# Moving half of a subtraction from VectorE to GpSimd for two resident operands of a transformer layer

## The chip, the cores and the metric

The kernel runs on one core of one Trainium2 chip. A core has five engines that run their own instruction queues and meet through semaphores: TensorE (PE in the profile; PEld is its weight load), VectorE (DVE), ScalarE (ACT), GpSimd (POOL) and SyncE (SP), which here issues nearly all DMAs. Working memory is SBUF (128 partitions); TensorE writes its sums to PSUM, in banks of 128x512; the inputs, the outputs and the intermediate results of the stages lie in HBM and are moved by DMA. The metric is the time of one execution on the device, in microseconds (us).

## The reference

One layer for 2048 tokens of width 1024, in float32: a token mixing step (sliding-window attention beside a gated linear recurrence), cross-attention into 256 memory tokens, and a SwiGLU feed-forward block of width 2816, each between two RMS norms with a residual.

```python
u = rms_norm(h, g_mix_pre)
z = u @ w_in                                   # 1024 x 2816
ya = swa_with_sinks(...)                       # columns of z
yh = hgrn2(...)                                # the others
y = concatenate([ya, yh]) @ w_out
h = h + rms_norm(y, g_mix_post)
u = rms_norm(h, g_x_pre)
m = rms_norm(mem, g_mem)
# cross-attention, 4 heads of 256, 256 memory tokens
q, k, v = u @ wq, m @ wk, m @ wv
y = (softmax(q k^T / 16) v) @ wo
h = h + rms_norm(y, g_x_post)
u = rms_norm(h, g_ffn_pre)
y = (silu(u @ w_gate) * (u @ w_up)) @ w_down
h = h + rms_norm(y, g_ffn_post)
```

## The kernel before

**Stages.** The first stage projects the tokens with `w_in`; the second runs the two kinds of token mixing and, beside them, folds the memory into two matrices: `qk` = wq k^T (1024x1024, heads by memory tokens) and `vo` = v wo. From there on one function, `phases` (line 1210), runs eight jobs one after the other, each a large matrix product: job 0 `w_out` (8 blocks of 256 tokens), job 1 the scores with `qk` (8 blocks), job 2 the values with `vo` (8), jobs 3 and 4 the hidden layer for the first and the second 1024 tokens (22 blocks each, 11 pairs of gate and up columns), jobs 5 to 7 the down projection in three slices of its depth. In every job one operand is *resident*: it stays in SBUF for all blocks. In job 1 that is `qk`, in job 3 the first half of the normalised tokens, transposed. The other operand is *streamed*, block by block.

**Seven products and three passes.** A block of a job is normally made as seven products in the manner of Strassen and Winograd (`seven`, line 1126): the resident operand is present as seven *parts*, sums and differences of its quarters, numbered 1 to 7, and a block uses them in the order 1, 5, 6, 3, 7, 2, 4. A last block of each job is made by quarters (`eight`) and uses an eighth part instead of some. Each part is held as two numbers, hi (the value rounded to the format of TensorE's faster float32 matmul) and lo = raw - hi, the rest; a product is then three matmuls for each of four slices of 128 rows (`products`, line 1114: hi by hi at line 1122, streamed hi by resident lo at 1123, streamed lo by resident hi at 1124). A step of a block is so twelve matmuls of 128x512.

**How a part is made.** `resident` (line 992) makes a part in two halves of two slices each. For each half a raw tile of 128x1024 is loaded to a buffer named `row`; then `split2` (line 982) lets ACT write hi (line 985) and DVE subtract (line 988) to give lo. Streamed tiles (`streamed`, line 1063) go through the same two lines, with tiles named S; some of their hi copies are made by POOL (line 987). In the profile resident parts are named T, streamed ones S.

**When a part is made.** There are seven slots for parts (four in the pool `big`, three in the pool `T`). `half` (line 1262) takes the next part of a queue as soon as a slot's last use has passed; so the parts of a job are made during the last block of the job before it and during its own first block, a stretch of some 60 us. Seven of the eight are made there, the eighth later. Rows are shared: nine `row` buffers hold raw halves, outputs of blocks and residuals, and a load to a row waits until its last reader is done.

**What else runs there.** At the same time the blocks of the job before end with their norms: DVE multiplies by the gain (lines 1520, 1595, 1608) and adds the residual (1521, 1599), ACT squares and sums (1471) and copies PSUM out (1137, 1375, 1495), POOL forms 1/sqrt (`rstds`, lines 1482 to 1486, the last one a `pow`), and TensorE transposes (1374). In the score blocks POOL also scales the row maxima (1554) for ACT's exponentials (1556).

**Order.** The instruction order on each engine isn't written by hand: a scheduler places the traced instructions by its own time model, so an instruction that changes its engine can also shift others near it. Within an engine's queue the order is then fixed; an instruction that waits holds up all behind it.

Of the kernel before, what the change touches and what calls it, by code (L numbers as in the profile page):

```python
# [15 lines left out]
ALU = mybir.AluOpType  # L16
# [20 lines left out]
def f32(ap):  # L37
    return ap.bitcast(F32)
# [10 lines left out]
class Layer:  # L49
# [929 lines left out]
    TAKES = {"s": (1,) * 7, "p": (2, 2, 0, 0), "q": (4, 0), "u": (2, 2), "v": (0, 0)}  # L979
    BLOCK = {1: (0, 0), 8: (0, 1), 2: (1, 0), 3: (1, 1)}  # L980

    def split2(self, raw, hi, lo, engine):

        if engine == "A":
            self.nc.scalar.activation(hi, raw, AF.Copy)  # L985
        else:
            self.nc.gpsimd.tensor_scalar(hi, raw, 1.0, 1.0, ALU.mult, ALU.mult)  # L987
        self.nc.vector.tensor_tensor(lo, raw, f32(hi), ALU.subtract)  # L988

    CHAIN = (5, 7, 6, 4)  # L990

    def resident(self, get, nk, key, dst, keep, sums):

        nc = self.nc
        halves = [(0, (nk + 1) // 2), ((nk + 1) // 2, nk)]

        def fetched(a, b):
            if key in self.BLOCK:  # L1000
                return get(*self.BLOCK[key], a, b - a), None
            if sums:
                return get(key, None, a, b - a), None
            if key == 5:
                return get(0, 1, a, b - a), get(0, 0, a, b - a)
            if key == 7:
                return get(1, 1, a, b - a), get(0, 1, a, b - a)
            if key == 6:
                return keep[7][len(src)], get(0, 0, a, b - a)
            return get(1, 0, a, b - a), keep[6][len(src)]  # L1010

        def split(a, b, t, o):
            if o is not None:
                nc.vector.tensor_tensor(t, t, o, ALU.add if key == 6 else ALU.subtract)
            self.split2(t, dst[:, 0, a:b], dst[:, 1, a:b], "A")

        src = []
        for a, b in halves:
            t, o = fetched(a, b)
            src.append(t)  # L1020
            if key in (6, 7):
                keep[key] = src
            yield lambda a=a, b=b, t=t, o=o: split(a, b, t, o)
# [186 lines left out]
    def phases(self, jobs, first, prologue=None):  # L1210
# [9 lines left out]
        for g, (n, i, p) in enumerate(steps):  # L1220
            key = (n, p, i > len(jobs[n][2]) // 2 if p == 8 else 0)
# [6 lines left out]
        T, keep = {}, [{} for _ in jobs]  # L1228
        current, left = [None], {}
        pending = []  # L1230
        if first:
            for i, p in enumerate(first):
                k = (0, p, False)
# [5 lines left out]
        def fetch(n, tile):  # L1239
            def get(i, j, a, c):  # L1240
                t = tile().rearrange("p (k d) -> p k d", d=512)[:, :c]
                if j is None:
                    self.load(t.rearrange("p k d -> p (k d)"), jobs[n][3][self.CHAIN.index(i), :, a * 512:(a + c) * 512])
                else:
                    jobs[n][0](t, i, j, a, c)
                return t

            return jobs[n][0] if first else get

        def lag(k):  # L1250
            return 2 if k[1] in self.BLOCK or jobs[k[0]][3] is not None else 0
# [10 lines left out]
        def half(g, tile):  # L1262

            if current[0] is None:
                if not queue:
                    return False
                free = min(slots, key=lambda s: s[1])
                if free[1] > g:
                    return False
                n, p, _ = k = queue.pop(0)  # L1270
                slots.remove(free)
                slots.append((free[0], uses[k][-1], free[2]))
                self._n += 1
                dst = (self.big if free[0] == "A" else self.tb).tile(
                    [P, 2, 4, 512], F32R, tag="big" if free[0] == "A" else "T", name=f"T_{self._n}",
                    bufs=4 if free[0] == "A" else 3)[:, :, :jobs[n][1]]
                T[k] = dst
                left[k] = 2
                current[:] = [(k, self.resident(fetch(n, tile), jobs[n][1], p, dst, keep[n], jobs[n][3] is not None)), 0]
            k, f = current[0]  # L1280
            pending.append((g + lag(k), k, next(f)))
            current[1] += 1
            if current[1] == 2:
                next(f, None)
                current[0] = None
            return True

        class Ready(dict):


            def __getitem__(_, p):
                q = next(q for q in range(g, len(steps)) if steps[q][2] == p)
                n, i, _ = steps[q]
                key = (n, p, i > len(jobs[n][2]) // 2 if p == 8 else 0)
                while left.get(key, 1):
                    if not split(len(steps)):
                        assert half(g - 1, self.row_tile), (g, key, queue[:3], slots)
                return T[key]
# [18 lines left out]
        if not first:  # L1317
            for i in range(8):
                half(-1, prologue)
                split(len(steps))  # L1320
                yield
# [9 lines left out]
        for _, nk, bl, _, beside in jobs:  # L1331
            for i, (kind, _, out, follow, addend) in enumerate(bl):
                stream(at + 1)
                after += [f() for f in beside.get(i, ())]
                run = (self.seven(ready, Ready(), nk, out, addend) if kind == "s" else
                       self.eight(ready, Ready(), nk, out) if kind == "p" else
                       self.plain(ready, Ready(), nk, out, addend, kind))
                for q in range(len(self.STEPS[kind])):
                    for _ in range(1 if g or not first else 3):
                        next(run)  # L1340
                        if first and g < 3:
                            yield
                    self.mark()
                    upto(need[g + 2])
                    if first and g == 1:
                        yield
                    for _ in range(1 if kind == "s" else 2):
                        for f in list(after):
                            if next(f, after) is after:
                                after.remove(f)  # L1350
                        if pending and lag(pending[0][1]):
                            with self.behind():
                                split(g)
                        else:
                            split(g)
                        if not first or g > 1:
                            half(g, self.row_tile)
                    g += 1
                after.append(follow())
                at += 1  # L1360
# [394 lines left out]
```

## Time and profile before

| | |
|---|---|
| median of three runs | 2598.62 us (2594.67 to 2599.31) |
| profiled execution | 2587.36 us, span of instructions 2585.7 us |
| TensorE busy, granted clock | 2548.3 us (99% of the span), 0.998 |
| DVE busy | 1747.9 us (68%) |
| ACT busy | 1261.0 us (49%) |
| POOL busy | 428.4 us (17%) |
| line 988 on DVE, resident parts made from rows | 120 instructions, 141.3 us |

The span is the time from the first to the last instruction. Busy times of different engines overlap. The rows of a timeline give start, duration, engine, line, operation, the tiles (written, then read), the shapes, and in brackets how long the engine was idle before and what released it. "x2" is two instructions merged to one row. Names of tiles are without their numbers, so a T in a row can be any part; which one it is follows from the order of instructions in the queue.

### The profile page before, as it was taken

The numbers are of one execution on the slowest core, as the hardware profiler recorded it, in microseconds if no ns is written. First come the engines' busy times: TensorE is split into PE (matmuls) and PEld (weight loads), VectorE is DVE, ScalarE is ACT, GpSimd is POOL, SyncE is SP. The second block draws the span as 40 slices with busy tenths as digits, with TensorE's granted clock in tenths as the row PEclk, the third lists the DMA queues.
The fourth block names the chain that finished last, engine by engine and source line by source line (L and its number), as shares of the span: only waits on it lengthen the run. The fifth ranks groups of instructions, "written<-read, shape, count | busy, mean of one in ns | idle before, by whom it ended". The sixth has DMA issues, their size and how long they took to land.

```text
span 2585.7 us, 34998 instructions
## 1 busy us (share of the span) xinstructions
PE 2548.3 (99%) x12371; PEld 2135.9 (83%) x12371; DVE 1747.9 (68%) x2759; ACT 1261.0 (49%) x2633; POOL 428.4 (17%) x612
## 2 busy tenths in 40 slices
PE   9999999999999999999999999999999999999998
PEld 8888888888988778888878888888888888888886
DVE  7785588986557778788876655576566556564656
ACT  5563466665555566465563333353333334443543
POOL 5231334321302232222300000000000000000022
PEclk9999999999999999999999999999999999999999
DMA  6445655855888886666963622253565444566888
GB/s 188 147 163 179 198 168 152 253 185 167 258 290 281 296 287 210 205 222 210 327 233 115 203 97 75 98 203 124 177 205 194 146 146 139 208 201 186 262 213 218
DMA packets 363663, 506.03 MB, mean 196 GB/s; under 512 B 20960, under 2 KB 249312, under 8 KB 363488
## 3 DMA queue, kind: packets, MB, share of 16 engines
q1 hardware_dynamic: 357440, 481.77, 56.5%
q0 software_dynamic: 6048, 22.02, 4.7%
q8 instruction: 97, 1.59, 0.2%
q14 instruction: 78, 0.64, 0.1%
HBM read 337.00 MB, written 166.72 MB: 195 GB/s over the span
## 4 chain that ended last, share of the span: by engine, by line
PE 83%; DMA 7%; DVE 4%; ACT 3%; issue 2%; POOL 1%; SPq 0%; DVEq 0%; POOLq 0%; ACTq 0%
PE psm L1122 23%; PE psm L1124 23%; PE psm L1123 22%; PE psg L156 2%; PE psg L157 2%; PE psg L158 2%; PE pss L1374 1%; DMA row<-y_d 1%; DMA raw<-in_wo_x_dram 1%; DMA u_d<-row 1%; DMA h1t_d<-row 1%; DMA row<-h_d 1%; ACT junk L1471 1%; ACT T L985 0%; PE pss L837 0%
## 5 line engine op out<-in xcount | busy, mean ns | idle before, releaser
L1122 PE MATMUL psm<-T,S 128*128 128x512 f32 x2695 | 1043.8, 391 | 11.0 <-ACT part L1137 6.5
L1123 PE MATMUL psm<-T,S 128*128 128x512 f32 x2695 | 1049.1, 390 | 2.1 <-DVE T L988 1.9
L1124 PE MATMUL psm<-T,S 128*128 128x512 f32 x2695 | 1038.9, 390 | 3.6 <-DVE S L988 3.6
L1122 PEld LDWEIGHTS psm<-T,S 128*128 128x128 f32 x2695 | 506.2, 188 | 120.3 <-ACT part L1137 7.0
L1124 PEld LDWEIGHTS psm<-T,S 128*128 128x128 f32 x2695 | 506.2, 188 | 110.4 <-DVE S L988 5.3
L1123 PEld LDWEIGHTS psm<-T,S 128*128 128x128 f32 x2695 | 506.5, 188 | 107.5 <-DVE T L988 4.1
L985 ACT ACTIVATE S<-sum 128x512 fp32r<-128x512 f32 (+1 forms) x314 | 188.7, 619 | 359.6 <-PE psm L1124 267.8
L988 DVE TENSOR_TENSOR S<-sraw,S 128x512 fp32r<-128x512 f32 (+1 forms) x319 | 217.0, 687 | 215.9 <-ACT S L985 201.8
L988 DVE TENSOR_TENSOR S<-sum,S 128x512 fp32r<-128x512 f32 (+1 forms) x372 | 249.7, 681 | 47.0 <-ACT S L985 31.8
L1137 ACT ACTIVATE part<-psm 128x512 f32<-128x512 f32 x273 | 161.7, 597 | 242.8 <-PE psm L1124 221.5
L985 ACT ACTIVATE S<-sraw 128x512 fp32r<-128x512 f32 (+1 forms) x272 | 167.4, 617 | 111.2 <-PE psm L1124 99.3
L1500 POOL DMA_DIRECT2D row<-y_d x28 | 25.7, 919 | 1111.4 <-DVE row L1686 1036.5
L988 DVE TENSOR_TENSOR T<-row,T 128x1024 fp32r<-128x1024 f32 (+1 forms) x120 | 141.3, 1192 | 60.9 <-ACT T L985 60.4
L1471 ACT ACTIVATE junk<-row 128x512 f32<-128x512 f32 x160 | 99.7, 625 | 60.5 <-DVE row L1493 30.0
L157 PE MATMUL psg<-u,whi 128*128 128x512 f32 x320 | 127.8, 399 | 0.0
L158 PE MATMUL psg<-u,wlo 128*128 128x512 f32 x320 | 127.1, 397 | 0.0
L156 PE MATMUL psg<-u,whi 128*128 128x512 f32 x320 | 127.1, 397 | 0.0
L985 ACT ACTIVATE T<-row 128x1024 fp32r<-128x1024 f32 x120 | 119.9, 1028 | 10.5 <-DMA row<-qk_s 3.5
L987 POOL TENSOR_SCALAR S<-sum 128x512 fp32r<-128x512 f32 x58 | 53.4, 921 | 294.6 <-PE psm L1124 237.2
L1637 DVE TENSOR_TENSOR row<-psm,part 128x512 f32<-128x512 f32 x66 | 43.7, 687 | 61.4 <-PE psm L1124 61.3
L1646 DVE TENSOR_TENSOR part<-psm,part 128x512 f32<-128x512 f32 x60 | 39.7, 687 | 62.4 <-PE psm L1124 62.2
L812 ACT ACTIVATE S<-S,w_mn 128x256 f32<-128x256 f32 (+1 forms) x128 | 63.1, 495 | 28.6 <-DVE w_mn L808 28.3
(363 smaller groups left out, 3679.1 us busy)
## 6 DMA issues: line engine op xcount, KB each, us to landing
sraw<-in_w_gate_dram SPq DMA_DIRECT2D x44, 512.0 KB, 3.7
sraw<-in_w_up_dram SPq DMA_DIRECT2D x44, 512.0 KB, 3.7
hid_d<-row SPq DMA_DIRECT2D x44, 512.0 KB, 2.7
h_d<-row SPq DMA_DIRECT2D x32, 512.0 KB, 4.8
y_d<-row SPq DMA_DIRECT2D x32, 512.0 KB, 3.3
sraw<-hid_d SPq DMA_DIRECT2D x32, 512.0 KB, 5.1
row<-y_d POOLq DMA_DIRECT2D x28, 512.0 KB, 7.1
sraw<-in_w_in_dram SPq DMA_DIRECT2D x44, 256.0 KB, 3.5
```

Of the source, the lines that this page charges most:

```text
L156: nc.tensor.matmul(ps, ah, bh, start=(i == 0), stop=False)
L157: nc.tensor.matmul(ps, ah, bl, start=False, stop=False)
L158: nc.tensor.matmul(ps, al, bh, start=False, stop=(i == n - 1))
L812: nc.scalar.activation(s[:, r, o:], s[:, r, o:], AF.Exp, bias=mn[:, i:i + 1], scale=-1.0, accum_out=den[:, i:i + 1])
L985: self.nc.scalar.activation(hi, raw, AF.Copy)
L987: self.nc.gpsimd.tensor_scalar(hi, raw, 1.0, 1.0, ALU.mult, ALU.mult)
L988: self.nc.vector.tensor_tensor(lo, raw, f32(hi), ALU.subtract)
L1122: nc.tensor.matmul(ps, s[:, 0, k, :], t[:, 0, k, :], start=st, stop=False, **kw)
L1123: nc.tensor.matmul(ps, s[:, 0, k, :], t[:, 1, k, :], start=False, stop=False, **kw)
L1124: nc.tensor.matmul(ps, s[:, 1, k, :], t[:, 0, k, :], start=False, stop=sp, **kw)
L1137: nc.scalar.activation(t, ps, AF.Copy)
L1471: self.nc.scalar.activation(junk, a, AF.Square, scale=float(D) ** -0.5, accum_out=to)
```

## The change

For job 1 and job 3, and only for the second half of each part, line 988's subtraction is issued to POOL (`nc.gpsimd`) instead of DVE. The hi copy stays on ACT. Eight parts in each of two jobs make sixteen instructions.

```diff
-    def split2(self, raw, hi, lo, engine):
+    def split2(self, raw, hi, lo, engine, rest=None):
         if engine == "A":
             self.nc.scalar.activation(hi, raw, AF.Copy)
         else:
             self.nc.gpsimd.tensor_scalar(hi, raw, 1.0, 1.0, ALU.mult, ALU.mult)
-        self.nc.vector.tensor_tensor(lo, raw, f32(hi), ALU.subtract)
+        (rest or self.nc.vector).tensor_tensor(lo, raw, f32(hi), ALU.subtract)
...
-    def resident(self, get, nk, key, dst, keep, sums):
+    def resident(self, get, nk, key, dst, keep, sums, shared):
...
-            self.split2(t, dst[:, 0, a:b], dst[:, 1, a:b], "A")
+            self.split2(t, dst[:, 0, a:b], dst[:, 1, a:b], "A", nc.gpsimd if shared and a else None)
...
-                current[:] = [(k, self.resident(fetch(n, tile), jobs[n][1], p, dst, keep[n], jobs[n][3] is not None)), 0]
+                current[:] = [(k, self.resident(fetch(n, tile), jobs[n][1], p, dst, keep[n], jobs[n][3] is not None,
+                                               n in (1, 3))), 0]
```

In the queues of the changed kernel as it is built, the moved subtractions stand on POOL behind the norms' `pow` of the same moment; around them some instructions of DVE, ACT, TensorE and SP have changed places with their neighbours, in the stretches where these two operands are made and nowhere else.

## The prediction

> **What bounds the kernel now.** I read the page's head first, then busy time by stretch for the two places where the touched parts are made, then TensorE's waits there, then the rows of the engines in those stretches.
>
> ```profile
> span 2585.7 us, 34998 instructions
> PE 2548.3 (99%) x12371; PEld 2135.9 (83%) x12371; DVE 1747.9 (68%) x2759; ACT 1261.0 (49%) x2633; POOL 428.4 (17%) x612
> ...
> 920.00:990.00 70.00, 64.66 (x304) 52.41 (x303) 54.00 (x68) 48.40 (x100) 23.00 (x29) 1.00 0.74 256
> 1270.00:1335.00 65.00, 61.84 (x282) 50.01 (x281) 54.55 (x61) 48.89 (x96) 10.17 (x16) 0.97 0.81 276
> ```
>
> TensorE is the bound. What an edit on DVE or POOL can win or lose is TensorE's idle time, and where these parts are made that is small: 70.00 - 64.66 = 5.3 us in the first stretch (columns: length, PE, PEld, DVE, ACT, POOL busy, PE clock) and 65.00 - 61.84 = 3.2 us in the second. The first holds the making of seven parts of the scores' operand, the second of seven parts of the first feed-forward operand; the eighth of each is made later. DVE is busy 77% and 84% of them.
>
> ```profile
> 959.93 0.50 PE L1123 MATMUL psm<-T,S 128*128 128x512 f32 x1 [0.92 <-DVE T L988]
> 962.76 0.47 PE L1122 MATMUL psm<-T,S 128*128 128x512 f32 x1 [1.41 <-ACT part L1137]
> 967.04 0.73 PE L1122 MATMUL psm<-T,S 128*128 128x512 f32 x2 [2.45 <-ACT T L985]
> ...
> 1305.44 0.50 PE L1122 MATMUL psm<-T,S 128*128 128x512 f32 x1 [2.04 <-ACT part L1137]
> 1306.24 0.40 PE L1122 MATMUL psm<-T,S 128*128 128x512 f32 x1
> 1306.47 0.48 PE L1123 MATMUL psm<-T,S 128*128 128x512 f32 x1
> 1306.75 0.63 PE L1124 MATMUL psm<-T,S 128*128 128x512 f32 x1
> 1309.74 0.54 PE L1122 MATMUL psm<-T,S 128*128 128x512 f32 x1
> ...
> 1323.71 0.50 PE L1123 MATMUL psm<-T,S 128*128 128x512 f32 x1 [0.24 <-DVE T L988]
> 1326.41 0.50 PE L1123 MATMUL psm<-T,S 128*128 128x512 f32 x1 [0.76 <-DVE T L988]
> ```
>
> These are the waits that an edit here can touch. Only three (0.92, 0.24, 0.76 us) end with the subtraction that moves; the large ones end with a copy or an eviction on ACT. After the 2.04 us gap matmuls start 0.23 us apart (1306.24 to 1306.47), and then 0.43: the seven from 1306.75 to 1309.74 take 2.99 us in place of 7 x 0.23, 1.4 us more. The 2.45 us gap had no such tail. The Trainium skill ("TensorE: Matmul & The Clock Gate", "What's actually happening") has the clock halve after an idle window of about 3.4 us; by that rule the 2.04 us gap alone would have had no tail, and here the row decides.
>
> **The change, part by part.** Sixteen subtractions lo = raw - hi of 128x1024 (two operands, eight parts, second halves) leave DVE and join POOL. Nothing is added or dropped; DMAs are the same in number.
>
> *Price of one.* DVE's is in the trace; POOL's of this shape isn't.
>
> ```profile
> L988 DVE TENSOR_TENSOR T<-row,T x120: 677/1218/1646, 788.6 to 2440.1; 128x1024 fp32r<-128x1024 f32 x112, 128x512 fp32r<-128x512 f32 x8
> L889 POOL TENSOR_TENSOR q<-qq,G x16: 1042/1046/2199, 268.9 to 704.8; 128x512 f32<-128x512 f32 x16
> L892 POOL TENSOR_TENSOR kk<-kk,G x16: 614/615/1164, 272.5 to 699.8; 128x256 f32<-128x256 f32 x16
> ```
>
> Two-input POOL medians are 0.615 us at 256 elements and 1.046 at 512, 0.431 us more per 256, so 1.046 + 2 x 0.431 = 1.91 us at 1024 (estimate). Ends: 1.05 us, the 512 row itself, and 2.09, its double. I take 1.91, which follows both rows. Against DVE's 1.22 each lo is 0.7 us longer once it starts. (The "GPSIMD Engine Reference" of the Trainium skill, "Elementwise — side-by-side cycle accounting", measures 4497 against 2293 ns at 2048; its ratio 1.96 would make this 2.4 us, an estimate, and add 0.5 us to each.)
>
> *Do the two engines hinder each other?*
>
> ```profile
> 1271.03 0.77 POOL L987 TENSOR_SCALAR S<-sraw 128x512 fp32r<-128x512 f32 x1 [3.38 <-PE psm L1124]
> 1271.24 1.63 DVE L988 TENSOR_TENSOR T<-row,T 128x1024 fp32r<-128x1024 f32 x1
> ...
> 961.44 4.05 POOL L987 TENSOR_SCALAR S<-sum 128x512 fp32r<-128x512 f32 x1 [5.22 <-PE psm L1124]
> ...
> 956.26 2.48 DVE L1520 SCALAR_TENSOR_TENSOR row<-row,q_r,g 128x1024 f32<-128x1024 f32 x2 [0.61 <-POOL q_r L1486]
> 958.66 2.35 DVE L988 TENSOR_TENSOR T<-row,T 128x1024 fp32r<-128x1024 f32 x2
> 960.93 2.35 DVE L1521 TENSOR_TENSOR row<-row,row 128x1024 f32<-128x1024 f32 x2
> 963.20 1.22 DVE L988 TENSOR_TENSOR T<-row,T 128x1024 fp32r<-128x1024 f32 x1
> 964.33 0.68 DVE L988 TENSOR_TENSOR S<-sraw,S 128x512 fp32r<-128x512 f32 x1
> ```
>
> They do. In the first pair DVE takes 1.63 us instead of 1.22 while a POOL copy runs; there the POOL copy took 0.77; the one at 961.44 lasts 4.05 and ends only after DVE's unbroken run of two-input work (to 965.01). So a moved subtraction first waits for DVE's current instruction (0 to 1.3 us, once 4.05 - 0.77 = 3.3), then holds DVE off for up to its 1.91 us. The Trainium skill ("SBUF — State Buffer", "Who interferes with whom") states why: a DVE instruction with two SBUF inputs and a GpSimd one that reads SBUF share one read interface, and the second to issue fully blocks. Both rows agree with it, and what it would do here is the second rival below. DVE gives up 1.13 us for each (its spacing: 960.93 to 963.20 holds two) and can be shut out for 1.91, a loss of 0.8 where it never rests. But it rests 16.0 and 10.5 us in the two stretches (70.00 - 54.00, 65.00 - 54.55), and what it loses there costs nothing.
>
> *First stretch.* The parts are used in the order 1, 5, 6, 3, 7, 2, 4.
>
> ```profile
> 949.95 0.33 SPq L75 DMA_DIRECT2D row<-qk_s  x1
> ...
> 954.23 1.06 ACT L985 ACTIVATE T<-row 128x1024 fp32r<-128x1024 f32 x1
> ...
> 957.65 8.26 DMA row<-qk_d
> ```
>
> Part 3's second lo is the first half of the pair at 958.66; its hi was ready at 955.29 (954.23 + 1.06), but two gain multiplies stood ahead, and TensorE waited 0.92 us. On POOL it follows a norm's pow and a copy of the streamed operand; with one DVE instruction to wait for it ends about 958.5 to 960.5, against 959.9. Either way the gain or loss is covered: TensorE next waits 1.41 and then until 967.04 for part 2's hi, whose raw half lands at 965.9 (957.65 + 8.26). So part 3: 0, as long as it loses under 1.41 + 2.45 us. In the changed kernel's order that load is issued ahead of a streamed tile's instead of behind it: I take 1.0 us off the 2.45 (bounds 0 and 2.45, the whole gap). Given back next: in ACT's new order the eviction that part 6 of the next block waits for stands behind part 2's second hi copy (1.06 us) and two exponentials; it was just in time before, so +1.0 (bounds 0 and 2.2). Part 2's second lo had no reserve, so it pays its 0.7, less what that eviction hides: +0.3 (bounds -0.4, its hi earlier, and 1.91). SP's raw loads wait for the moved subtractions to free their rows; the one at 949.95 followed part 6's, which is about as early on POOL: 0. Sum +0.3.
>
> *Second stretch.*
>
> ```profile
> 1283.74 1.01 POOL L1486 TENSOR_TENSOR q_r<-q_w,mhalf 128x2 f32<-128x2 f32 x1
> 1285.24 2.47 DVE L1595 SCALAR_TENSOR_TENSOR row<-row,q_r,g 128x1024 f32<-128x1024 f32 x2
> 1287.63 1.21 DVE L988 TENSOR_TENSOR T<-row,T 128x1024 fp32r<-128x1024 f32 x1
> 1288.77 2.35 DVE L1599 TENSOR_TENSOR row<-row,row 128x1024 f32<-128x1024 f32 x2
> ...
> 1290.02 0.60 ACT L1495 ACTIVATE row<-psm 128x512 f32<-128x512 f32 x1 [1.57 <-DVE row L1599]
> ...
> 1302.89 2.02 ACT L985 ACTIVATE T<-row 128x1024 fp32r<-128x1024 f32 x2
> 1304.79 1.08 ACT L1137 ACTIVATE part<-psm 128x512 f32<-128x512 f32 x2
> ...
> 1290.02:1304.79 14.77, 13.27 (x66) 10.69 (x64) 11.82 (x14) 14.74 (x31) 2.66 (x6) 1.00 0.93 322
> ```
>
> Part 1's second lo now stands on POOL right behind this pow (end 1284.75), when DVE starts the two multiplies. If it slips in between them, the first addition of L1599 ends at 1284.8 + 2 x 1.2 + 1.9 + 1.2 + 1.2 = 1291.5 instead of 1290.0; ACT waits for it and then works without rest (14.74 of 14.77 us) until the eviction at 1304.79, so the gap before 1305.44 grows by about 1.4. If DVE holds on, it shrinks by 0.4. I take +1.2. On the other side, part 3's second lo waited 4.3 us in DVE's queue (hi 1302.89 + 2.02, lo 1309.23), and its row frees this load:
>
> ```profile
> 1309.23 2.35 DVE L988 TENSOR_TENSOR T<-row,T 128x1024 fp32r<-128x1024 f32 x2
> ...
> 1310.48 6.45 DMA row<-h_d
> 1317.03 0.10 DVE row L1599
> ```
>
> On POOL it ends near 1308.5; the load, the addition, the silu and part 2's hi behind it come up to 2 us earlier, which takes the 0.24 and most of the 0.76: -0.8 (bounds -1.0, both, and 0). Part 2's extra 0.7 goes into that lead: 0. Sum +0.4.
>
> The eighth parts are made from about 1100 and 1700 on. From 1095 to 1160 TensorE's whole list of waits is one line, and from 1640 to 1760 it is empty:
>
> ```profile
> PE psm L1122 <- ACT part L1137: 0.6, 1, 0.6
> ```
>
> So they are hidden by the work of running blocks: 0. If that cover were gone each would cost its extra 0.7. POOL's norm steps and copies of the streamed operand now queue behind the moved work; they feed products or row scalings that come later than the part itself, so I give them 0 beyond the pow and multiplies counted above.
>
> Sum: 0.3 + 0.4 = +0.7 us on the profiled execution's 2587.36 (span 2585.70). The three runs' median, 2598.62, lies 11.3 above it; on that scale 2599.3. Adding all upper bounds (2.2 + 1.91 + 1.4) gives +5.5, all lower ones (-2.45 - 0.4 - 0.4 - 1.0) -4.3: the forecast's own range is 2594 to 2604. A measurement of this kernel can tell about 0.2%, 5.2 us, from no change.
>
> **Rivals.** *Slower: POOL is shut out at part 3.* DVE's run from 956.26 to 965.0 has no pause, and the row at 961.44 shows POOL kept out to the end of such a run. In the new order it loses two moved subtractions (2.3) and gains two streamed ones (1.2): to 963.9. Part 3's second lo would end at 963.9 + 1.9 = 965.8, 5.9 late; less the later waits of 1.41 and 2.45, +2.0; part 7's second lo follows on POOL, +1.9; a gap of that length brings a half-rate tail, +1.4; with the sum's 0.7 some 6 us, 2604.6. It begins to count once part 3 ends later than 959.9 + 3.9 = 963.8. For it: that row. Against: the one at 1271, where POOL came in between two DVE instructions.
>
> *Slower: DVE is shut out each time.* If DVE paces both stretches, 14 x 0.8 = 11 us: 2610. For it: loads of 54.00 + 7 x 0.8 = 59.6 us of 70 and 60.1 of 65 leave little rest. Against: the rest that is left, and that TensorE's large waits end with ACT. This is what the Trainium skill's full block (the page named above) comes to at its worst.
>
> *Faster: the gaps close.* If DVE, rid of 14 x 1.2 us, feeds ACT earlier, the 2.45 us gap goes with the earlier load and the 2.04 goes with its 1.4 tail: -5.9, 2593. For it: DVE at 84%. Against: the 2.04 gap ends with ACT, which is busy without a rest for 14 us before it.
>
> *It doesn't do what it says:* POOL merely replaces DVE as the last arriver, and nothing else moves. Same time, held in the forecast.
>
> **How the numbers follow.** Forecast (within 0.2%) 0.43; POOL shut out 0.20; DVE shut out 0.13; gaps closed 0.24. The time is the forecast's, 2599.3. The range reaches over the slow rivals' times and, by the bounds of the first stretch, some 4 us past the fast one's: 2589 to 2611 leaves about 0.2 out.
>
> **What would show it.** Right: sixteen POOL rows of L988 near 1.9 us or longer; DVE's T group down by 16; a wait of TensorE for POOL at part 2 under 1 us; the gap before the first feed-forward block's part 6 near 3 us. Wrong: POOL rows of 4 us or more at part 3 with a TensorE wait of 4 us behind them; or the two large gaps gone.

## The result, and the profile after

The changed kernel is slower: 2603.95 us median against 2596.29 for the kernel before on the same chip, ratio 1.0029 with a 95% interval of 1.0022 to 1.0037, that is 7.5 us. The profiled execution took 2597.38 us (span 2595.6), where the one before took 2587.36. Line numbers of the changed kernel are one or two higher: its matmuls are L1123 to L1125 (L1122 to L1124 before), transposes L1376 (L1374), the norms' pow L1488 (L1486), the gain multiplies L1522, L1597 and L1610 (L1520, L1595, L1608).

The head of the page, then busy time by stretch (length, PE, PEld, DVE, ACT, POOL, PE clock), both of the changed kernel:

```profile
span 2595.6 us, 35006 instructions
PE 2549.0 (98%) x12371; PEld 2135.9 (82%) x12371; DVE 1756.1 (68%) x2743; ACT 1259.5 (49%) x2633; POOL 462.5 (18%) x628
```

```profile
920.00:990.00 70.00, 63.11 (x291) 51.27 (x290) 54.66 (x53) 45.77 (x95) 31.89 (x34) 0.98 0.74 252
1270.00:1335.00 65.00, 57.93 (x272) 47.25 (x272) 53.01 (x51) 44.75 (x87) 25.91 (x20) 1.00 0.87 291
```

TensorE's busy time hardly moved (2548.3 to 2549.0); its idle time did, and in the two stretches named: 6.9 us idle instead of 5.3, and 7.1 instead of 3.2. These are 5.5 of the 9.2 us by which it grew between the two profiled executions; of the rest 1.8 us lie ahead of 900 us, where the change touches nothing, and 1.4 between 1100 and 1270, and they are not followed here. DVE was to get lighter by sixteen subtractions of 1.22 us, 19.5 us; its busy time went up by 8.2 us (1747.9 to 1756.1), and in the first stretch it issues fewer instructions (53 records for 68) in more time. The two groups of L988 that changed, by instruction group (count, shortest/median/longest in ns):

```profile
L988 DVE TENSOR_TENSOR T<-row,T x104: 678/1218/3414, 790.2 to 2449.0; 128x1024 fp32r<-128x1024 f32 x96, 128x512 fp32r<-128x512 f32 x8
...
L988 POOL TENSOR_TENSOR T<-row,T x16: 2352/2406/3381, 935.6 to 1715.7; 128x1024 fp32r<-128x1024 f32 x16
```

All sixteen moved, at a median of 2.41 us, and DVE's longest row of this kind grew from 1.65 to 3.41 us. What that does in the second stretch, rows of four engines of the changed kernel in order of time (start, duration, engine, line; in brackets the idle time before and what ended it):

```profile
1290.38 2.40 POOL L988 TENSOR_TENSOR T<-row,T 128x1024 fp32r<-128x1024 f32 x1
...
1290.45 4.61 DVE L1597 SCALAR_TENSOR_TENSOR row<-row,q_r,g 128x1024 f32<-128x1024 f32 x2 [0.91 <-POOL q_r L1488]
...
1297.36 0.60 ACT L1497 ACTIVATE row<-psm 128x512 f32<-128x512 f32 x1 [1.93 <-DVE row L1601]
...
1306.21 2.49 POOL L988 TENSOR_TENSOR T<-row,T 128x1024 fp32r<-128x1024 f32 x1 [2.82 <-ACT T L985]
...
1306.55 0.19 ACT L1473 ACTIVATION_READ_ACCUMULATOR junk<-row 128x1 f32 x1
...
1308.67 0.64 POOL L1484 TENSOR_TENSOR q_v<-q_s 128x2 f32<-128x2 f32 x1
...
1311.19 2.48 DVE L1610 SCALAR_TENSOR_TENSOR row<-row,q_r,extra 128x1024 f32<-128x1024 f32 x2 [0.60 <-POOL q_r L1488]
...
1312.62 1.06 PE L1376 MATMUL pss<-ident,row 128*128 128x128 f32 x8 [3.42 <-DVE row L1610]
...
1313.98 0.39 PE L1125 MATMUL psm<-T,S 128*128 128x512 f32 x1
1314.21 0.40 PE L1123 MATMUL psm<-T,S 128*128 128x512 f32 x1
1314.22 6.25 POOL L988 TENSOR_TENSOR T<-row,T 128x1024 fp32r<-128x1024 f32 x2
...
1314.80 3.41 DVE L988 TENSOR_TENSOR T<-row,T 128x1024 fp32r<-128x1024 f32 x1
...
1318.26 0.50 PE L1124 MATMUL psm<-T,S 128*128 128x512 f32 x1 [1.60 <-DVE T L988]
```

The same sum of squares, first small step and transposes in the kernel before:

```profile
1299.06 0.20 ACT L1471 ACTIVATION_READ_ACCUMULATOR junk<-row 128x1 f32 x1
...
1299.34 0.20 POOL L1482 TENSOR_TENSOR q_v<-q_s 128x2 f32<-128x2 f32 x1 [14.58 <-ACT junk L1471]
...
1302.33 1.06 PE L1374 MATMUL pss<-ident,row 128*128 128x128 f32 x8
```

Two things stand here. At 1290.38 part 1's subtraction starts on POOL, right behind the pow, and the two gain multiplies that the same pow releases take 4.61 us; before, the same pair took 2.47 (its row at 1285.24 in the prediction). At 1306.74 the sum of squares of the next norm is ready (1306.55 + 0.19), but POOL is in part 6's subtraction until 1308.70, so the norm's first small step starts at 1308.67, 1.9 us late; before, it followed the sum by 0.08 us. The row that both feed comes late, and TensorE, which works in its own order, waits 3.42 us ahead of its transposes; no such wait was there before. The 2.04 us gap is gone, and this one stands in its place. From 1314.22 parts 3 and 7 read on POOL, a subtraction that DVE kept takes 3.41 us for 1.22, and TensorE waits 1.60 us for it. Behind the gap of 3.42 us matmuls start 0.23 us apart (1313.98 to 1314.21): it has no half-rate tail.

The first stretch, in the same form (the pair that part 1 meets in the kernel before, then the changed kernel):

```profile
934.99 2.48 DVE L1520 SCALAR_TENSOR_TENSOR row<-row,q_r,g 128x1024 f32<-128x1024 f32 x2
```

```profile
935.58 2.40 POOL L988 TENSOR_TENSOR T<-row,T 128x1024 fp32r<-128x1024 f32 x1
...
935.64 4.62 DVE L1522 SCALAR_TENSOR_TENSOR row<-row,q_r,g 128x1024 f32<-128x1024 f32 x2 [1.78 <-POOL q_r L1488]
...
958.91 4.94 DVE L1522 SCALAR_TENSOR_TENSOR row<-row,q_r,g 128x1024 f32<-128x1024 f32 x2 [1.19 <-POOL q_r L1488]
...
959.45 3.32 POOL L988 TENSOR_TENSOR T<-row,T 128x1024 fp32r<-128x1024 f32 x1
...
962.83 0.50 PE L1124 MATMUL psm<-T,S 128*128 128x512 f32 x1 [1.37 <-POOL T L988]
...
968.92 1.29 PE L1376 MATMUL pss<-ident,row 128*128 128x128 f32 x8 [3.65 <-DVE row L1523]
...
970.56 0.63 PE L1125 MATMUL psm<-T,S 128*128 128x512 f32 x1
...
970.98 0.63 PE L1123 MATMUL psm<-T,S 128*128 128x512 f32 x1
```

Here too a pair of gain multiplies is held by part 1, at 935.6, and the next norm's by part 3, at 958.9 (2.48 us each before, the second at 956.26 in the prediction). TensorE waits 1.37 us for part 3's lo, and 3.65 us for a normed row ahead of transposes; behind that gap matmuls start 0.42 us apart (970.56 to 970.98), the half-rate tail that the prediction saw behind the 2.04 us gap.

### The profile page after: what moved, and what is told of

Its sections match the earlier page's. It is cut to its first block, busy times and chain, and to the rows that moved or that the text cites. A ratio compares the mean times of both kernels' runs of the same rounds, so it can differ in the third digit from the quotient of the medians.

```text
span 2595.6 us, 35006 instructions
## 1 busy us (share of the span) xinstructions
PE 2549.0 (98%) x12371; PEld 2135.9 (82%) x12371; DVE 1756.1 (68%) x2743; ACT 1259.5 (49%) x2633; POOL 462.5 (18%) x628
## 4 chain that ended last, share of the span: by engine, by line
PE 81%; DMA 7%; DVE 4%; issue 3%; ACT 2%; POOL 2%; SPq 1%; DVEq 0%; POOLq 0%; ACTq 0%
PE psm L1123 23%; PE psm L1125 22%; PE psm L1124 22%; PE psg L158 2%; PE psg L157 2%; PE psg L156 2%; PE pss L1376 1%; DMA row<-y_d 1%; DMA kk<-z_d 1%; DMA z<-in_w_out_dram 1%; DMA raw<-in_wo_x_dram 0%; DMA u_d<-row 0%; POOL T L988 0%; DMA x<-in_w_out_dram 0%; DMA y_d<-sg 0%
## 5 line engine op out<-in xcount | busy, mean ns | idle before, releaser
L1124 PE MATMUL psm<-T,S 128*128 128x512 f32 x2695 | 1049.6, 390 | 5.1 <-DVE T L988 3.4
L1123 PE MATMUL psm<-T,S 128*128 128x512 f32 x2695 | 1043.3, 392 | 7.8 <-ACT part L1138 5.0
L1125 PE MATMUL psm<-T,S 128*128 128x512 f32 x2695 | 1039.9, 390 | 4.3 <-DVE S L988 4.3
L1123 PEld LDWEIGHTS psm<-T,S 128*128 128x128 f32 x2695 | 506.9, 188 | 116.6 <-ACT part L1138 7.4
L1124 PEld LDWEIGHTS psm<-T,S 128*128 128x128 f32 x2695 | 506.6, 188 | 111.1 <-DVE T L988 5.0
L1125 PEld LDWEIGHTS psm<-T,S 128*128 128x128 f32 x2695 | 506.5, 188 | 111.1 <-DVE S L988 6.0
L988 DVE TENSOR_TENSOR S<-sraw,S 128x512 fp32r<-128x512 f32 (+1 forms) x319 | 221.4, 702 | 212.6 <-ACT S L985 199.9
L988 DVE TENSOR_TENSOR S<-sum,S 128x512 fp32r<-128x512 f32 (+1 forms) x372 | 255.1, 695 | 52.2 <-ACT S L985 36.2
L988 DVE TENSOR_TENSOR T<-row,T 128x1024 fp32r<-128x1024 f32 (+1 forms) x104 | 125.5, 1221 | 56.0 <-ACT T L985 55.7
L988 POOL TENSOR_TENSOR T<-row,T 128x1024 fp32r<-128x1024 f32 x16 | 41.1, 2571 | 411.6 <-ACT T L985 411.6
```

The source lines that it names most:

```text
L988: (rest or self.nc.vector).tensor_tensor(lo, raw, f32(hi), ALU.subtract)
L1123: nc.tensor.matmul(ps, s[:, 0, k, :], t[:, 0, k, :], start=st, stop=False, **kw)
L1124: nc.tensor.matmul(ps, s[:, 0, k, :], t[:, 1, k, :], start=False, stop=False, **kw)
L1125: nc.tensor.matmul(ps, s[:, 1, k, :], t[:, 0, k, :], start=False, stop=sp, **kw)
```

## The experiments

Theory A: while POOL reads for a moved subtraction, DVE's two-input work stands still; norms come late, and TensorE waits where its order puts a late row. Rival B: the planner's new order of TensorE's instructions (the transposes stand earlier) costs it. Rival C: the moved lo itself arrives late at its matmul. Rival D: POOL's queue, in which small steps now stand behind 2.4 us of other work. Every ratio is to the kernel before, run beside it.

**One operand at a time.** The edit of the first; the second has `n == 3`:

```diff
-                                               n in (1, 3))), 0]
+                                               n == 1)), 0]
```

> Only the scores' operand has its second halves subtracted by POOL; the first feed-forward operand is made as before. The trace of the changed kernel put about 2.7 us of its loss into the first stretch, 2.8 us between the stretches and 3.1 us into the second. Theory A (each POOL subtraction keeps DVE off while it reads, the norms that DVE makes come late, and TensorE waits at their transposes): a loss of its own in each stretch, so 2.7 to 5.5 us over the kernel before here, a ratio of 1.001 to 1.002, with the wait of some 3.6 us for L1523 still there. Theory B (the changed order of TensorE's instructions costs it, not DVE): the same place and the same 2.7 us, since the order around part 7 changes here as well. Theory C (the moved subtraction itself arrives late): waits for POOL's L988 add up to the loss; they were 1.4 us in the first stretch. If the loss sits in the second stretch alone: ratio 1.000.

> Only the first feed-forward operand has its second halves subtracted by POOL. Theories A and B: 3.1 us over the kernel before (ratio 1.0012), with the wait of some 3.4 us for L1610 at the transposes and the first stretch as before. By A the two parts' losses add up to that of the changed kernel, 7.5 us. By C: the waits for POOL's L988, 0.3 us in this stretch, are all of it: ratio 1.0001.

Scores' operand alone: 1.0017 (1.0006 to 1.0028). Feed-forward operand alone: 1.0012 (1.0001 to 1.0023). Together they make 1.0029, so the losses add, as far as intervals of 0.0011 to either side tell, and each stretch has its own. TensorE's waits in the first stretch of the one and the second stretch of the other:

```profile
PE pss L1376 <- DVE row L1523: 3.0, 1, 3.0
```

```profile
PE pss L1376 <- DVE row L1610: 4.6, 1, 4.6
```

Waits for POOL's own result were 1.3 and 0.3 us, less than the loss in both: C does not carry it. A and B are not told apart.

**The order of TensorE.** The changed kernel with one row tile's transposes held behind part 7's seventh matmul (`pin` is that matmul):

```diff
-                self.transposed(y[i], y[i])
+                self.transposed(y[i], y[i], pin if n == 14 and not i else ())
...
-                nc.tensor.transpose(...)
+                with self.queued(*pin): nc.tensor.transpose(...)
```

> The changed kernel, but the eight transposes of one normed row tile (the last mixed block's first) may stand on TensorE only behind the seventh of part 7's twelve matmuls, close to where they stood before the change; it moved them ahead of eleven of the twelve. Theory B: the wait of 3.6 us ahead of them and the half-rate matmuls behind it go, so 2.7 us of the 7.5 come back, ratio to the kernel before 1.0018. Theory A: the row is as late as it was; only the work that now stands ahead, six matmuls of 0.23 us, 1.4 us, comes off the wait: 2.2 us of it stay, ratio 1.0023 to 1.0029.

1.0040 (1.0025 to 1.0056): nothing came back. The transposes went back six of the eleven places that the change had moved them (5202 of TensorE's instructions stand ahead of them before, 5191 in the changed kernel, 5197 here), so this run alone does not clear the order. The traces do the rest: in both runs of the next experiment the same transposes stand at 5191, without a wait and without a loss, and in the second stretch the ones that wait stand at 6774 before as after the change. B falls. In this run the wait for the row is gone, and another took its place, larger than either theory had. POOL, DVE and TensorE, in that order:

```profile
971.54 3.15 POOL L988 TENSOR_TENSOR T<-row,T 128x1024 fp32r<-128x1024 f32 x1 [2.47 <-ACT T L985]
...
972.42 3.36 DVE L988 TENSOR_TENSOR T<-row,T 128x1024 fp32r<-128x1024 f32 x1
...
975.84 0.79 PE L1124 MATMUL psm<-T,S 128*128 128x512 f32 x1 [3.33 <-DVE T L988]
```

A subtraction that stayed on DVE is held behind one that moved, and now that is what TensorE lacks.

**POOL without the reading.** First POOL only writes (zeros in place of these lo halves; the matmuls on them start 0.23 us apart as before); then it writes two and a half times, so that it is busy as long as with the subtraction:

```diff
-        (rest or self.nc.vector).tensor_tensor(lo, raw, f32(hi), ALU.subtract)
+        if rest:   # the second run has three memsets, the last of half the tile
+            rest.tensor_tensor(lo[:, :, 0:1], raw[:, :, 0:1], f32(hi)[:, :, 0:1], ALU.subtract)
+            rest.memset(f32(lo), 0.0)
+        else: self.nc.vector.tensor_tensor(lo, raw, f32(hi), ALU.subtract)
```

> POOL in place of the moved subtractions subtracts one column of 4 or 2 elements per row and then fills lo with zeros: the writes and the wait for hi are left, nearly all of the reading and the arithmetic are left out (so lo is zero in these halves). Theory A: without the reading DVE is not held off, its pairs of gain multiplies take 2.5 us again and not 4.6, the waits of 3.6 and 3.4 us at the transposes go: no slower than the kernel before, ratio 0.998 to 1.000. Theory B: the order of the instructions is changed here as well; if it is the cause, waits of 2 us or more at the transposes stay and the ratio stays above 1.001.

> In place of each moved subtraction POOL subtracts one column (0.20 us in the run that only wrote) and then fills lo with zeros two and a half times (0.95 us each there), so about 2.5 us of POOL's time, as long as the subtraction's 2.4, with hardly any reading; lo is zero in these halves. Theory A (the reading keeps DVE off): no loss, ratio 0.998 to 1.000, DVE's pairs of gain multiplies near 2.5 us. Rival D (POOL's queue: the norms' small steps and the streamed copies stand behind 2.4 us of other work, and the reading is beside the point): the loss stays, ratio 1.002 to 1.003, with waits of 3 us at the transposes.

Written once: 0.9986 (0.9973 to 0.9999). Busy as long, without the reading: 0.9989 (0.9977 to 1.0001). The second is the test. DVE's pair and POOL's work beside it, in the second stretch:

```profile
1291.25 2.48 DVE L1597 SCALAR_TENSOR_TENSOR row<-row,q_r,g 128x1024 f32<-128x1024 f32 x2
...
1291.44 2.56 POOL L988 MEMSET T<- 128x1024 f32 x3
```

POOL is busy for 2.56 us right beside the pair, as the subtraction was for 2.40, and the pair takes 2.48 us and not 4.61. The loss is gone. POOL's queue is as full as in the changed kernel, and TensorE still waits 2.3 us for L1610 there, so D is real as a wait; without the reading it makes no net loss (the 2.04 us wait for ACT is not in that trace). The reading is the cause, together with the arithmetic on what is read, which both runs leave out with it.

**Smaller and more.** Each moved subtraction in four pieces, or done twice:

```diff
+        if rest:                          # four_pieces
+            for d in range(0, 512, 128):
+                rest.tensor_tensor(lo[:, :, d:d + 128], raw[:, :, d:d + 128], f32(hi)[:, :, d:d + 128], ALU.subtract)
+        else: self.nc.vector.tensor_tensor(lo, raw, f32(hi), ALU.subtract)
...
+        for _ in range(2 if rest else 1): # subtracted_twice
+            (rest or self.nc.vector).tensor_tensor(lo, raw, f32(hi), ALU.subtract)
```

> POOL makes each moved subtraction as four of 128x256, about 0.6 us each by the row of that width, 2.4 us in all. If a DVE instruction is held only until POOL's current instruction ends and gets in between two pieces, a pair of gain multiplies takes at most 2.5 + 2 x 0.6 = 3.7 us and the loss shrinks to about a half, ratio 1.0015. If POOL's next piece gets in first, the pair takes 4.6 us or more and the ratio stays at 1.003.

> POOL does each moved subtraction twice over (same result, 16 more reads of 2.4 us). Theory A and rival D: the loss about doubles, 15 us, ratio 1.006 (more if TensorE's gaps become long enough for a lower clock). If the loss came from the changed order alone (theory B), it stays near 7.5 us, 1.003.

Four pieces: 1.0026 (1.0015 to 1.0038). The pair shrank as the first case said, to 3.44 us, and the loss did not, as the second said. Part 1 and the pair in the second stretch, POOL and then DVE:

```profile
1297.27 5.77 POOL L988 TENSOR_TENSOR T<-row,T 128x256 fp32r<-128x256 f32 x4
...
1297.32 3.44 DVE L1597 SCALAR_TENSOR_TENSOR row<-row,q_r,g 128x1024 f32<-128x1024 f32 x2 [0.60 <-POOL q_r L1488]
```

The rows fit two engines that take turns piece by piece, so that the cost is shared out: DVE is held 1.0 us instead of 2.1, and POOL's four pieces, 4 x 0.72 us at the shortest, take 5.77. TensorE then waits 4.0 us for POOL's lo in the first stretch, in three waits (1.4 in the changed kernel), and 5.4 for L1610.

Twice: 1.0130 (1.0111 to 1.0149), some 34 us, more than four times the change's loss where twice was expected. A and D had only the sign of that. Part of the excess is TensorE's clock, which is lower in both stretches (the column before the last two; 0.98 and 1.00 in the changed kernel above):

```profile
920.00:990.00 70.00, 59.63 (x264) 47.85 (x262) 57.53 (x42) 38.34 (x76) 45.66 (x35) 0.95 0.75 253
1270.00:1345.00 75.00, 65.53 (x299) 53.18 (x298) 65.49 (x60) 47.07 (x97) 40.96 (x31) 0.95 0.84 279
```

The mean granted clock of these runs is 0.991, against 0.996 of the kernel before beside them; over 2593 us that is some 13 of the 34 us (an estimate). That the slack which takes the first reads no longer takes the second is likely for the others, and was not tried.

**The reading by itself.** DVE makes every lo as before, and POOL subtracts besides, into the dead raw half:

```diff
-        (rest or self.nc.vector).tensor_tensor(lo, raw, f32(hi), ALU.subtract)
+        self.nc.vector.tensor_tensor(lo, raw, f32(hi), ALU.subtract)
+        rest and rest.tensor_tensor(raw, raw, f32(hi), ALU.subtract)
```

> The move is undone: DVE makes every lo as before the change, and nothing that TensorE uses comes from POOL; but POOL subtracts too, behind DVE, into the raw half, which nobody reads again (the half comes free for the next load up to some 2.4 us later). Theory A: the reads keep DVE off as in the changed kernel and DVE has its old work besides: at least its 7.5 us, and about 11 with the 3.6 that the run that only wrote had gained, ratio 1.003 to 1.0045. Theories B and C (order, late lo): the consumer is as before, ratio 1.000 to 1.001.

1.0090 (1.0075 to 1.0104), some 23 us: nothing that TensorE uses was moved, and the loss is three times the change's. B and C are out as causes of the whole. It is twice what A expected. The mean granted clock is 0.9925 against 0.9969 beside it, over 2594 us some 11 us (an estimate), about what is above the expectation; that rows come free later may be part of it as well, and was not separated.

**Which parts.** By the condition on `key`: parts 1, 5 and 6; parts 3, 7, 2 and 4; the eighth alone; part 1 alone.

```diff
-            self.split2(t, dst[:, 0, a:b], dst[:, 1, a:b], "A", nc.gpsimd if shared and a else None)
+            self.split2(t, dst[:, 0, a:b], dst[:, 1, a:b], "A", nc.gpsimd if shared and a and key in (1, 5, 6) else None)
```

> POOL makes only the second half of the eighth part of either operand; the other fourteen stay with DVE, and the instructions on every engine stand nearly as before the change. By the prediction's zero for the eighth parts, and by theory A, since DVE and TensorE have other work there that covers it: ratio 1.000, 0.999 to 1.001, and TensorE's waits in the two stretches as before the change (2.5 and 2.0 us for ACT).

> POOL makes the second halves of parts 1, 5 and 6 of both operands; parts 3, 7, 2, 4 and the eighth stay with DVE. In the changed kernel's trace POOL's reads of these three lengthen DVE's work by about 2.1 + 2.0 us in the first stretch (pair of gain multiplies 4.6 for 2.5, a streamed subtraction 2.7 for 0.7) and 2.1 + 0.8 in the second, 7.0 of some 21.7 us. Theory A, if the loss goes by the time that DVE is kept off: 7.5 x 7.0 / 21.7 = 2.4 us, ratio 1.001. If these three are used early enough to have slack: 1.000 or under.

> POOL makes the second halves of parts 3, 7, 2 and 4 of both operands; the others stay with DVE. Their reads lengthen DVE's work by about 6.5 us in the first stretch and 8.2 in the second, 14.7 of some 21.7 us. Theory A: 7.5 x 14.7 / 21.7 = 5.1 us, ratio 1.002. If the early parts carry the loss: 1.000.

> POOL makes only the second half of part 1 of either operand. The run with the first three parts lost all that the changed kernel loses, and its trace offers two mechanisms: part 1's read starts right behind a norm's pow and holds the second of that norm's two gain multiplies (the pair takes 4.6 for 2.5 us, in both stretches), and part 6's stands in front of the next norm's small steps on POOL (their sums were ready at 1310.4, q_v started at 1312.28, 1.9 us later). If the held pair carries it: 2.1 us in either stretch or somewhat more, ratio 1.0015 to 1.002, with the pairs at 4.6 us and a wait at the transposes of the second stretch near 2.5 us. If part 6's place on POOL or its hold carries it: ratio 1.000 to 1.0005 and no wait for L1610 of more than 1 us.

| POOL makes | moved | ratio | interval |
|---|---|---|---|
| the eighth parts | 2 | 0.9995 | 0.9982 to 1.0007 |
| 1, 5, 6 | 6 | 1.0036 | 1.0023 to 1.0049 |
| 3, 7, 2, 4 | 8 | 1.0006 | 0.9994 to 1.0018 |
| 1 | 2 | 1.0018 | 1.0007 to 1.0028 |

The share by DVE's held time was wrong, and clearly: the four parts with two thirds of it cost nothing that can be told, the three with one third cost as much as the whole change. Two subtractions of sixteen, part 1's, make some 60% of it by the middle value; the interval reaches from a quarter to nearly all. The second stretch with part 1 alone, POOL, DVE and TensorE:

```profile
1288.06 2.39 POOL L988 TENSOR_TENSOR T<-row,T 128x1024 fp32r<-128x1024 f32 x1
...
1288.12 4.61 DVE L1597 SCALAR_TENSOR_TENSOR row<-row,q_r,g 128x1024 f32<-128x1024 f32 x2
...
1308.19 1.06 PE L1376 MATMUL pss<-ident,row 128*128 128x128 f32 x8 [2.59 <-ACT junk L1473]
```

So the held pair is enough here: 2.1 us on DVE at 1288 are a wait of 2.59 us 20 us later, at the transposes of the next norm (the profile names ACT's sum of squares in its chain as the last to come). The wait for ACT right behind them is 1.35 us, where it was 2.04, so some 1.9 us are new. With parts 5 and 6 moved as well (ACT, POOL and TensorE in the run of the first three):

```profile
1310.17 0.20 ACT L1473 ACTIVATION_READ_ACCUMULATOR junk<-row 128x1 f32 x1
...
1312.28 0.64 POOL L1484 TENSOR_TENSOR q_v<-q_s 128x2 f32<-128x2 f32 x1
...
1316.23 1.94 PE L1376 MATMUL pss<-ident,row 128*128 128x128 f32 x8 [4.73 <-DVE row L1610]
```

The sum is ready at 1310.37 and POOL takes it up at 1312.28, behind part 6's subtraction; TensorE's wait goes from 2.59 to 4.73 us. That these 1.9 us are part 6's is read from the trace; part 6 was not moved alone. In the first stretch no single part explains the loss: TensorE's listed waits from 920 to 1000 us sum to 5.2 us before, 6.9 in the changed kernel, 4.6 with part 1 alone, 6.3 with parts 1, 5 and 6 (the largest, 4.3 us, for a copy by ACT and not for L1523) and 3.5 with 3, 7, 2 and 4. Its pair is held in the run of part 1 too (4.61 us), so which holds make its 4.4 us stays open. No version that was run beats the kernel before while it computes every lo.

## Why the prediction was right or wrong

The predicted 2599.3 us is 4.7 under the measured median, and 2589 to 2611 holds it; the likeliest case, within 0.2%, did not come true. The number flatters the sum. It said +0.7 us and 7.5 were measured, outside of its own bounds of -4.3 to +5.5; the time came nearer because the three runs that it started from had a median of 2598.62, 2.3 us above that of the kernel before beside the changed one, and the range holds it because it was stretched over the slow rivals.

- **Price of one.** 1.91 us was wrong, and so was its upper end, 2.09: 2.41 measured. From 512 elements (1.046 us) to 1024 it grows by 1.36 us, where the two smaller rows gave 2 x 0.431. The ratio cited from the "GPSIMD Engine Reference" of the Trainium skill, "Elementwise — side-by-side cycle accounting", 1.96, gave 2.4 as an estimate; the trace's 2.41 / 1.22 = 1.98 agrees.
- **Do the engines hinder each other.** Right, and more than priced: a hold is POOL's whole read, 2.1 us of 2.4 on the pair, and not 0.8 net. "SBUF — State Buffer", "Who interferes with whom", in the Trainium skill says full block between two-input DVE work and a GpSimd read; the pairs of 4.61 with the reading and 2.48 with as long a write agree.
- **DVE's rest of 16.0 and 10.5 us, in which a loss costs nothing.** This is the step that failed. The rest is a sum over a stretch; what counts is which instruction is held. Parts 3, 7, 2 and 4 held DVE longest at 1.0006; part 1 held it 2.1 us, on the chain of a norm, at 1.0018.
- **First stretch, +0.3.** Measured alone: 1.0017, 4.4 us. Part 3 was followed with care and came out as said (late by little, TensorE waits 1.37 us, inside the bound); part 1, whose subtraction meets the pair at 935.6, has no term in the sum, nor has the hold of the next pair by part 3's own read. How much of the loss is each one's is not shown.
- **Second stretch, +0.4.** Measured alone: 1.0012, 3.1 us. Part 1's term had the right mechanism, POOL slipping in at the gain multiplies, and half its size: 1.2 for 2.1 on the pair and some 1.9 at TensorE. Its path was another too: the sum put it on the gap ahead of part 6, which ends with an eviction by ACT; it came at the transposes of the next norm. It starts 0.07 us ahead of the first multiply (1290.38, 1290.45), not between the two. Of the gain of 0.8 from part 3's earlier row a part can be seen: at the same two matmuls the wait of 0.24 is 0.30 (now for POOL) and that of 0.76 is no longer listed, with TensorE itself later. But two new waits for subtractions that DVE kept, 1.60 and 1.75 us, stand ahead of them, where there was none.
- **POOL's norm steps behind the moved work, 0.** Wrong at part 6: 1.9 us in front of a norm's first step. Where POOL did not read, a wait of 2.3 us at the same place made no net loss; on top of the held pair it did.
- **The eighth parts, 0.** Right: 0.9995.
- **What was to show it.** The sixteen rows and DVE's count came as named, and TensorE's wait for POOL at part 2 is 0.3 us; the gap near 3 us came as 3.42, but at the transposes and not at part 6.
- **Rivals.** POOL shut out at part 3 did not happen: no POOL row of 4 us at part 3, and the lo there ended at 962.77, under the 963.8 from which it would count, although the changed kernel is already later by then. DVE shut out each time is the right mechanism at the wrong places; its 11 us suppose that every hold counts, and eight of fourteen count for next to nothing. Gaps closed: both large gaps did go, which the prediction would have read as a gain, and others of 3.65 and 3.42 us took their place. Relief of DVE is worth something only without the reading (0.9986, which still owes its lo).

## What to carry to other kernels

Here work of two inputs that was moved from VectorE to GpSimd did not relieve VectorE: each read of 2.40 us held a pair of two-input instructions for 2.1 us, and VectorE's busy time rose by 8.2 us. Price such a move as a hold of GpSimd's whole instruction on the two-input work that VectorE has next, and look up what that is. A share of idle time doesn't answer that: the hold that was seen to cost is the one on a chain (in the second stretch pow, gain multiplies, sum of squares, next norm, transposes), and an instruction that stands right behind the event that starts the chain, as part 1's behind the pow, met it in both stretches. On the engine that receives the work, look for small steps of such a chain queued behind it.

## What the runs showed of the hardware

A GpSimd write of 2.56 us beside VectorE's two-input pair cost the pair nothing (2.48 us), where a two-input read of 2.40 us cost it 2.1 us. Shorter GpSimd reads shared the cost out: four pieces of 0.72 us at the shortest stretched to 5.77 us together, and the pair to 3.44. Doubling the reads took the loss from 0.29% to 1.30%. The length of a gap in TensorE's work did not alone decide whether half-rate matmuls came behind it: gaps of 2.04 and 3.65 us had them (0.43 and 0.42 us apart for 0.23), gaps of 2.45 and 3.42 us had none.
